# Holding the matmul engine's instructions of a hybrid decoder layer to the order of the source

## The chip, the cores and the metric

One core of a Trainium2 chip runs the whole kernel. The metric is the device time of one execution in microseconds (us). The engines are called as the profile calls them: PE (matrix products; PEld is its weight load), DVE (vector), ACT (scalar), POOL (GpSimd) and SP, which here only issues DMA transfers. Each engine works through its own list of instructions in the order of that list, and waits by semaphores for others.

## The reference

One decoder layer, 1024 positions, width 1024, all in float32:

```
h    = rmsnorm(x)
proj = h @ w_in              # q, k, v of 8 forgetting heads, 8 forget logits,
                             # q, k, v of 8 stick-breaking heads
o_fox = softmax(q.k/8 + F[t] - F[s], s <= t) @ v,  F = cumsum(log sigmoid(forget logit + bias))
o_sb  = A @ v,  A[t,s] = sigmoid(z[t,s]) * prod_{s<j<t}(1 - sigmoid(z[t,j])),  z = q.k/8, s < t
x = x + concat(rmsnorm(o_fox), rmsnorm(o_sb)) @ w_out
u = causal_dwconv3(rmsnorm(x) @ w_up);  gate, val = split(u)
x = x + (silu(gate) * val) @ w_down
return rmsnorm(x)
```

## The kernel before, in words

Every float32 product is made of three matmuls on a high and a low part of each operand (`mm3`, lines 158 to 161). The high part is a rounded copy (mostly by ACT), the low part the difference (by DVE or POOL), so a product's three matmuls need work of two other engines first.

**Attention.** The 16 heads come two by two. For a block of 128 queries `score` (line 449) makes the products of q and k, in tiles `s` of up to 512 columns (lines 466 and 467; line 470 adds the causal mask on the diagonal). The pool of `s` has three buffers. For a forgetting head DVE reads the tile at line 475, adding the row `fbt` (the cumulated forget gate, fetched from DRAM at line 444), ACT takes the exponential, DVE the reciprocal of the sum (line 488) and POOL scales the weights `w` (line 489). For a stick-breaking head ACT makes two sigmoids (lines 480 and 481), DVE a running product (line 493) and POOL the weights (line 494). `trans` (line 497) turns 128x128 pieces of `w` on PE (line 505) into `tp`; ACT copies the high part (line 513, `ph` or `pth`) and DVE makes the low one (line 514, `pl` or `ptl`). `pv` (line 517) multiplies by v: pairs of matmuls, high (line 525) and low (line 526).

**What sets the order.** `attention_stream` (line 566) yields these pieces with a cost each; a second stream, `fill_stream` (line 661), yields the projections of later heads (`qk_unit`, whose products are lines 159 to 161 on `pj`, and `v_quarter`, lines 277 to 279), the forget gate and its scan (`forget_scan`, line 319, with eight small transposes at line 326, whose result goes to DRAM and comes back as `fbt`), and at the end `open_out` (line 620) and the forgetting heads' part of the out-projection (`fox_out`, line 639, products of `ogh` and `ogl` with the weights). The loop at lines 692 to 701 emits them interleaved: before an attention piece, so much of the fill as LEAD + RATE x (cost so far) allows. `open_out` spreads the group norm (`group_spread`, line 601) and loads the attention outputs of the forgetting heads (`load_og`, line 607: ACT line 616, DVE line 617).

Emission is not yet the order in which an engine works. A scheduler of the framework orders the instructions of each engine afterwards, by its own estimate of when each is ready; only engines named in `manual_schedule` (line 72) keep the order of emission. Before, that is SP alone.

**After attention.** The rest of the out-projection and the second norm follow (`norm_cols`, line 744: sums of squares by matmuls of one column, line 748; `norm_rows`, line 754: `spread`, line 182, turns the reciprocal roots `rr` of line 175 into a row on PE at line 184, and ACT copies it to `rbc`). `first` and `second` (lines 829 and 834) make two products of the up-projection early for its first three blocks, emitted as first(0), `norm_cols`, `norm_rows`, first(1), first(2), second(0) to second(2). The up- and down-projection then take, block by block, seven products of sums of quarter matrices in place of eight (`product`, line 817; the loop at line 1059; the names in PORD), whose operands are made by DVE, POOL and ACT (`produce`, line 891, with the low part at line 906) a few products ahead. The final norm in three column parts is woven into the last products by `events` (line 1194).

Of the kernel before, what the change touches and what calls it, by code (L numbers as in the profile page):

```python
# [68 lines left out]
def layer(ctx, tc, xT, wqk, wv0, wv, wout, wup, wdn, cols, fbias, yT):  # L69
    nc = tc.nc  # L70
    act = nc.scalar.activation
    ctx.enter_context(tc.manual_schedule(engines={mybir.EngineType.SP}))

    const = ctx.enter_context(tc.tile_pool(name="const", bufs=1))
    dram = ctx.enter_context(tc.tile_pool(name="dram", bufs=1, space=DRAM))
# [1219 lines left out]
```

## Time and profile before

| | us |
|---|---|
| median of 3 runs | 1442.43 (1439.91 to 1442.75) |
| the profiled execution, its own time | 1441.58 |
| its span in the profile | 1439.6 |
| PE busy | 1317.6 (92%) |
| DVE busy | 1116.7 (78%) |
| POOL busy | 859.4 (60%) |
| ACT busy | 620.8 (43%) |

The span begins with the first instruction that the profile shows; the execution's own time is 2.0 us longer. Times in the rows below count from the span's start. The stretches of the kernel: the first norm and the first projections to about 81 us, attention to about 645, the rest of the out-projection and the second norm to about 740, the up-projection to about 1200, the down-projection and last norm to the end. The granted clock is the share of TensorE's full rate: 1.00 is 2.4 GHz and 0.50 is 1.2 GHz.

### The profile page before, as it was taken

What the parts mean: (1) busy time and instruction counts of PE and PEld (TensorE: products, weight loads), DVE (VectorE), ACT (ScalarE), POOL (GpSimd) and SP (SyncE); (2) the same over time, 40 slices, a digit from 0 to 9 for tenths busy, and PEclk for the clock granted to TensorE, in tenths of its full rate; (3) what the DMA queues carried; (4) which work ended last, traced back from release to release, by engine and by line L of the source; (5) the groups of instructions that cost most, each with busy time, mean ns of one, the idle gap of its engine ahead of it and who ended that gap; (6) DMA issues with size and microseconds to landing.
All of it is one profiled execution on the core that took longest, in us unless ns stands there. A gap on an engine that the chain in (4) does not pass through costs nothing.

```text
span 1439.6 us, 19147 instructions
## 1 busy us (share of the span) xinstructions
PE 1317.6 (92%) x6640; PEld 1075.9 (75%) x6640; DVE 1116.7 (78%) x1588; ACT 620.8 (43%) x1128; POOL 859.4 (60%) x730
## 2 busy tenths in 40 slices
PE   7899999999898887889778899999999998999995
PEld 5878878877787765777556688888888865878785
DVE  6246555655676677786899999998888889899987
ACT  5134434444454554353443434443443354344334
POOL 7344454543747573455667788878878763454423
PEclk9999999999999999999889999999999998999997
DMA  5556555545444454547311233333322355554313
GB/s 179 183 161 187 152 154 163 147 147 135 149 121 124 119 159 143 179 147 270 125 44 59 84 106 110 110 110 110 110 97 95 96 176 204 180 171 132 126 36 117
DMA packets 97232, 194.89 MB, mean 135 GB/s; under 512 B 8680, under 2 KB 35688, under 8 KB 97136
## 3 DMA queue, kind: packets, MB, share of 16 engines
q1 hardware_dynamic: 96272, 193.04, 42.6%
q8 instruction: 52, 0.85, 0.3%
q10 hardware_dynamic: 864, 0.64, 0.1%
q14 instruction: 44, 0.36, 0.1%
HBM read 132.79 MB, written 60.85 MB: 135 GB/s over the span
## 4 chain that ended last, share of the span: by engine, by line
PE 50%; DMA 18%; DVE 16%; POOL 7%; issue 6%; SPq 2%; ACT 2%; DVEq 0%; POOLq 0%; ACTq 0%
PE u L161 8%; PE u L160 8%; PE u L159 8%; PE pj L159 5%; PE pj L161 5%; PE pj L160 5%; DMA q<-qkd 4%; DVE fbt L493 3%; DMA vd<-vs 3%; DMA wraw<-in_wqk_dram 2%; DMA wraw<-in_wv_dram 2%; PE tp L505 2%; DMA fbt<-nfd 2%; PE o L526 2%; PE o L525 1%
## 5 line engine op out<-in xcount | busy, mean ns | idle before, releaser
L143 POOL TENSOR_TENSOR wl<-wraw,wh 128x256 fp32r<-128x256 f32 (+2 forms) x134 | 125.3, 952 | 26.9 <-ACT wh L140 21.3
L494 POOL TENSOR_TENSOR w<-w,fbt 128x128 f32<-128x128 f32 (+3 forms) x64 | 90.1, 1417 | 84.4 <-DVE fbt L493 59.9
L904 ACT CAST wh<-s 128x512 fp32r<-128x512 f32 (+1 forms) x136 | 79.8, 591 | 125.7 <-POOL s L879 71.0
L493 DVE TENSOR_TENSOR_SCAN fbt<-fbt 128x128 f32<-128x128 f32 (+3 forms) x64 | 103.5, 1624 | 25.9 <-ACT fbt L480 22.0
L142 POOL TENSOR_SCALAR wh<-wraw 128x256 fp32r<-128x256 f32 (+1 forms) x112 | 55.3, 509 | 108.8 <-DMA wraw<-in_wqk_dram 60.7
L878 POOL TENSOR_TENSOR s<-wraw 128x512 f32<-128x512 f32 (+1 forms) x34 | 55.8, 1641 | 96.0 <-DVE wl L906 53.5
L505 PE MATMUL tp<-ident,w 128*128 128x128 f32 x576 | 94.0, 281 | 19.5 <-DVE pl L514 9.5
L159 PE MATMUL pj<-xh,wh 128*128 128x512 f32 x224 | 103.1, 460 | 5.1 <-DVE yf L293 5.1
L906 POOL TENSOR_TENSOR wl<-wraw,wh 128x512 fp32r<-128x512 f32 x60 | 102.9, 1722 | 0.6 <-ACT wh L904 0.6
L505 PEld LDWEIGHTS tp<-ident,w 128*128 128x128 f32 x576 | 70.7, 144 | 39.1 <-DVE pl L514 12.6
L906 POOL TENSOR_TENSOR wl<-s,wh 128x512 fp32r<-128x512 f32 x48 | 88.5, 1845 | 13.8 <-ACT wh L904 13.4
L514 DVE TENSOR_TENSOR pl<-tp,ph 128x512 fp32r<-128x512 f32 x96 | 64.9, 685 | 40.9 <-ACT ph L513 40.5
L161 PE MATMUL pj<-xh,wl 128*128 128x512 f32 x224 | 91.9, 410 | 0.0
L160 PE MATMUL pj<-xl,wh 128*128 128x512 f32 x224 | 91.3, 407 | 0.0
L485 ACT ACTIVATE w<-w,m 128x128 f32<-128x128 f32 (+3 forms) x64 | 49.7, 776 | 91.1 <-DVE m L475 86.0
L1003 DVE SCALAR_TENSOR_TENSOR tg<-ua,col,tg 128x1023 f32<-128x1023 f32 (+1 forms) x44 | 88.1, 2002 | 0.0
L480 ACT ACTIVATE fbt<-s 128x512 f32<-128x512 f32 (+2 forms) x96 | 47.8, 498 | 83.8 <-PE s L470 39.2
L489 POOL TENSOR_SCALAR w<-w,l 128x128 f32<-128x128 f32 (+3 forms) x64 | 47.6, 748 | 59.9 <-DVE l L488 32.7
L904 ACT CAST wh<-wraw 128x512 fp32r<-128x512 f32 (+1 forms) x96 | 55.1, 589 | 63.1 <-DMA wraw<-in_wdn_dram 25.0
L1003 DVE SCALAR_TENSOR_TENSOR tv<-ub,col,tv 128x1023 f32<-128x1023 f32 (+1 forms) x44 | 76.0, 1727 | 5.7 <-ACT tv L1001 5.6
L513 ACT CAST ph<-tp 128x512 fp32r<-128x512 f32 x96 | 55.7, 590 | 53.1 <-PE o L525 33.4
L885 POOL TENSOR_TENSOR s<-wraw 128x512 f32<-128x512 f32 (+1 forms) x34 | 56.4, 1658 | 35.7 <-DVE wl L906 33.4
(409 smaller groups left out, 4569.4 us busy)
## 6 DMA issues: line engine op xcount, KB each, us to landing
wraw<-in_wup_dram SPq DMA_DIRECT2D x47, 512.0 KB, 3.6
qkd<-hl SPq DMA_DIRECT2D x32, 512.0 KB, 2.9
td<-tg SPq DMA_DIRECT2D x44, 256.0 KB, 2.3
vd<-vs SPq DMA_DIRECT2D x32, 256.0 KB, 4.5
q<-qkd SPq DMA_DIRECT2D x16, 512.0 KB
kh<-qkd SPq DMA_DIRECT2D x32, 256.0 KB, 16.6
kl<-qkd SPq DMA_DIRECT2D x32, 256.0 KB, 17.4
vt<-vd SPq DMA_DIRECT2D x16, 512.0 KB, 17.9
```

Of the source, the lines that this page charges most:

```text
L143: nc.gpsimd.tensor_tensor(self.lo[:, sl], self.raw[:, sl], f32(self.hi[:, sl]), ALU.subtract)
L159: nc.tensor.matmul(ps, ah, bh, start=start, stop=False)
L160: nc.tensor.matmul(ps, ah, bl, start=False, stop=False)
L161: nc.tensor.matmul(ps, al, bh, start=False, stop=stop)
L493: nc.vector.tensor_tensor_scan(qt[:, rev], qt[:, rev], qt[:, rev], 1.0, ALU.mult, ALU.bypass)
L494: nc.gpsimd.tensor_tensor(w[:, :n], w[:, :n], qt[:, T - n + 1:T + 1], ALU.mult)
L505: nc.tensor.transpose(tp[:, a * 256 + b * P:a * 256 + (b + 1) * P], ws[2 * g + b][:, kb * P:(kb + 1) * P], ident)
L514: nc.vector.tensor_tensor(pl[:, z:], tp[:, z:], f32(ph[:, z:]), ALU.subtract)
L885: nc.gpsimd.tensor_tensor(d["s3"], g[:, :w], v[:, :w], ALU.subtract)
L904: nc.scalar.copy(h[:, o:o + w], src)
L906: eng.tensor_tensor(l[:, o:o + w], src, f32(h[:, o:o + w]), ALU.subtract)
L1003: nc.vector.scalar_tensor_tensor(t[:, s:], us[:, :T - s], col[:, cw + tap:cw + tap + 1], t[:, s:], op0=ALU.mult, op1=ALU.add)
```

## The change

PE is added to the engines whose instructions keep the order in which the source emits them. No instruction is added or removed; SP's list is the same; the lists of DVE, ACT and POOL, which the scheduler still orders, shift at many places.

```diff
-    ctx.enter_context(tc.manual_schedule(engines={mybir.EngineType.SP}))
+    ctx.enter_context(tc.manual_schedule(engines={mybir.EngineType.SP, mybir.EngineType.PE}))
```

The first place is on PE at the start of attention, where the value projection (lines 277 to 279) begins; `s` are score tiles and `tp` the turned weights. Before:

```order
L467 MATMUL s<-kl,q 128x384
L470 LDWEIGHTS identb
L470 MATMUL s<-mask_f,identb 128x128
L159 MATMUL pj<-xh_239,wh 128x512
L160 MATMUL pj<-xl_247,wh 128x512
L161 MATMUL pj<-xh_239,wl 128x512
L277 MATMUL pj<-wh,xh_232 128x256
L278 MATMUL pj<-wl,xh_232 128x256
L279 MATMUL pj<-wh,xl_240 128x256
```

And in the changed kernel:

```order
L467 MATMUL s<-kl,q 128x384
L470 LDWEIGHTS identb
L470 MATMUL s<-mask_f,identb 128x128
L466 MATMUL s<-kh,q 128x512
L467 MATMUL s<-kl,q 128x512
L470 LDWEIGHTS identb
L470 MATMUL s<-mask_f,identb 128x128
L159 MATMUL pj<-xh_239,wh 128x512
L160 MATMUL pj<-xl_247,wh 128x512
L161 MATMUL pj<-xh_239,wl 128x512
L505 MATMUL tp<-ident,w 128x128 x3
L277 MATMUL pj<-wh,xh_232 128x256
```

The fourth score tile (512 columns wide) now follows the third one directly, and the first three transposes come ahead of the value projection; before, both came after 26 matmuls of it.

The second place is on PE a little later, and stands for 24 places like it in attention: four score matmuls between two of the pairs of lines 525 and 526.

```order
 L525 MATMUL o<-ph,vt 128x256
+L526 MATMUL o<-pl,vt 128x256
+L525 MATMUL o<-ph,vt 128x256
+L526 MATMUL o<-pl,vt 128x256
+L525 MATMUL o<-pth_576,vt 128x256
+L526 MATMUL o<-ptl_577,vt 128x256
+L525 MATMUL o<-pth_576,vt 128x256
+L526 MATMUL o<-ptl_577,vt 128x256
 L466 MATMUL s<-kh,q 128x384
 L467 MATMUL s<-kl,q 128x384
 L466 MATMUL s<-kh,q 128x256
 L467 MATMUL s<-kl,q 128x256
```

The four score matmuls stood right behind the first high product; now all eight matmuls of the pairs come ahead of them.

The third place is on PE in the second norm: `sq` are the squares whose sums go before, `b21h` an operand of the first up-projection products, `rr` the reciprocal roots.

```order
 L748 MATMUL u<-ones,sq 128x1
-L161 MATMUL pj<-b21h_7184,wl 128x512
-L159 MATMUL pj<-b21h_7186,wh 128x512
-L160 MATMUL pj<-b21l_7187,wh 128x512
-L161 MATMUL pj<-b21h_7186,wl 128x512
-L159 MATMUL pj<-b21h_7188,wh 128x512
-L160 MATMUL pj<-b21l_7189,wh 128x512
-L161 MATMUL pj<-b21h_7188,wl 128x512
 L184 MATMUL u<-ident,rr 128x128 x4
```

Seven matmuls (and two more between the sums, further up) no longer stand ahead of the spread of `rr`; they come behind the products `first(1)` and `first(2)`.

## Rows read from the trace of the kernel before

**Rows 1.** The page: span; busy time of the engines.
```profile
span 1439.6 us, 19147 instructions
PE 1317.6 (92%) x6640; PEld 1075.9 (75%) x6640; DVE 1116.7 (78%) x1588; ACT 620.8 (43%) x1128; POOL 859.4 (60%) x730
```

**Rows 2.** Stretches: length; busy PE, PEld, DVE, ACT, POOL; granted clock, DMA share, GB/s.
```profile
480.00:520.00 40.00, 37.40 (x199) 30.60 (x200) 26.20 (x34) 18.72 (x40) 30.52 (x30) 0.91 0.49 136
520.00:560.00 40.00, 27.27 (x162) 21.36 (x161) 33.74 (x37) 22.79 (x47) 17.87 (x12) 0.95 0.53 159
720.00:760.00 40.00, 29.85 (x100) 20.43 (x98) 36.74 (x41) 17.91 (x31) 28.41 (x13) 0.83 0.12 40
```

**Rows 3.** Waits of PE: line waiting, its releaser, total us, times, longest.
```profile
PE o L526 <- DVE pl L514: 11.5, 7, 3.2
PE s L466 <- DMA kh<-qkd: 7.1, 1, 7.1
```

**Rows 4.** Timeline of PE: start us, us, instruction, [idle before <-releaser].
```profile
73.02 0.77 PE L159 MATMUL pj<-xh,wh 128*128 128x512 f32 x1 [5.06 <-DVE yf L293]
...
93.30 0.33 PE L466 MATMUL s<-kh,q 128*128 128x384 f32 x1
...
94.47 0.27 PE L277 MATMUL pj<-wh,xh 128*128 128x256 f32 x1
...
97.41 0.28 PE L278 MATMUL pj<-wl,xh 128*128 128x256 f32 x1
98.68 0.51 PE L466 MATMUL s<-kh,q 128*128 128x512 f32 x1 [0.99 <-DVE m L475]
...
101.28 0.55 PE L505 MATMUL tp<-ident,w 128*128 128x128 f32 x3
```

**Rows 5.** Timelines of DVE and of POOL, 98 to 101 us.
```profile
98.32 0.29 DVE L475 CUSTOM_DVE_ANT_0 w<-s,fbt 128x128 f32<-128x128 f32 x1 [2.96 <-DMA fbt<-nfd]
...
100.75 1.04 POOL L489 TENSOR_SCALAR w<-w,l 128x256 f32<-128x256 f32 x2 [0.29 <-DVE l L488]
```

**Rows 6.** Stretches of PE alone: length, PE busy us, granted clock, DMA share, GB/s.
```profile
74.00:78.00 4.00, 4.00 (x11) 0.50 0.85 279
96.00:101.00 5.00, 4.01 (x27) 1.00 1.00 267
559.00:563.00 4.00, 4.00 (x19) 0.50 0.17 54
```

**Rows 7.** Timeline of PE around the first pairs of lines 525 and 526.
```profile
106.24 0.34 PE L466 MATMUL s<-kh,q 128*128 128x384 f32 x1
...
106.83 0.32 PE L526 MATMUL o<-pl,vt 128*128 128x256 f32 x1
```

**Rows 8.** Timeline of PE at the first scores of the new head.
```profile
558.31 1.08 PE L466 MATMUL s<-kh,q 128*128 128x256 f32 x3 [7.12 <-DMA kh<-qkd]
```

**Rows 9.** Chain that ended last: start us, us, what.
```profile
540.50 17.61 DMA kh<-qkd
```

**Rows 10.** Timelines of PE and of DVE at the second norm's spread.
```profile
721.63 1.05 PE L184 MATMUL u<-ident,rr 128*128 128x128 f32 x4
...
719.92 0.16 DVE L175 TENSOR_TENSOR rr<-rs_s,rs_t 128x4 f32<-128x4 f32 x1
723.34 3.59 DVE L765 SCALAR_TENSOR_TENSOR x<-x,col,rbc 128x512 f32<-128x512 f32 x2 [3.26 <-ACT rbc L757]
```

**Rows 11.** Timeline of PE at the start of the up-projection.
```profile
760.86 0.64 PE L161 MATMUL pj<-t4h,wl 128*128 128x512 f32 x1 [3.02 <-POOL wl L906]
```

**Rows 12.** Timelines of PE and DVE, down-projection and last norm.
```profile
1207.79 0.79 PE L160 MATMUL u<-b22l,wh 128*128 128x512 f32 x1 [1.08 <-POOL b22l L761]
...
1411.30 0.28 PE L161 MATMUL pj<-b21h,wl 128*128 128x256 f32 x1
...
1413.78 0.60 PE L184 MATMUL pj<-ident,rr 128*128 128x128 f32 x4
...
1413.48 0.15 DVE L175 TENSOR_TENSOR rr<-rs_s,rs_t 128x4 f32<-128x4 f32 x1
```

## Prediction

> **What bounds the kernel now.** I read the page first: of a span of 1439.6 us the matmul engine (PE) is busy 1317.6 [rows 1], so it idles 122 us, and nothing that only fills those waits better or worse can be worth more. I then cut the span into stretches of 40 us [rows 2]. In attention PE idles a little (2.6 us of 40 at 480); from 720 to 760 it is busy 29.85 and VectorE (DVE) 36.74, so there DVE is the bound. The list of what PE waited for [rows 3] says that the large sums belong to attention: the low halves of the weights that line 514 makes on DVE (11.5 us), and one wait of 7.1 us for a key transfer. PE starts its matmuls one after the other, so a waiting one holds all that stand behind it. A change of PE's order alone can therefore act in two ways only: it moves work out of a wait, or into one.
>
> The order of instructions says where PE's order differs: six pieces at the start of attention (A), 24 small swaps through attention (B), ten pieces around the opening of the out-projection (C), and then one spot each in the second norm (D), the start of the up-projection (E), the first block of the down-projection (F) and the end (G). No instruction is added or dropped, and SP's order is the same; DVE, ScalarE and POOL are still ordered by the framework and shift somewhat in response.
>
> **A, the first scores.** A score tile has three buffers. Before, the third score starts at 93.30, and then 26 matmuls of the value projection run from 94.47 to 97.53, one every 0.118 us; only after a wait of 0.99 us comes score four, at 98.68 [rows 4], because DVE begins on the first score at 98.32, held by the transfer of the forget row [rows 5]. Now score four stands directly behind score three, ahead of three projection matmuls of line 159 to 161, and the first three transposes stand ahead of the 26. So PE stops at about 93.7 and goes on at 98.68: 5.0 us. Score four and the three matmuls take about 1.3 us, to 100.0. The transposes cannot start sooner than at 101.28, as before, since POOL's weights for them come from 100.75 on [rows 5]: another 1.3 us. Together 6.3 us of waiting in place of 0.99, so **+5.3 us**; the 3 us of value projection are still owed afterwards. Two early scores no longer stand between the transposes of the forget scan (line 326), so the forget row may set out up to 0.6 us sooner (two scores of two steps of 0.118 each, and their masks), which makes it **+4.7**. Then the clock: after the 5.06 us wait that ends at 73.02 [rows 4], PE's granted clock from 74 to 78 was 0.50, that is 1.2 GHz, over 4.00 us of work [rows 6], half of which, 2.0, is loss. The 0.99 us wait lies in a stretch with a granted clock of 1.00. The bounds are +3 (the lower value with later waits taking some back) and +7.3 (5.3 + 2.0). I take **+5**, nearer the wait that is counted than the clock that may or may not fall. The Trainium skill (TensorE: Matmul & The Clock Gate, section HAM oscillation) says that a wait between bursts sets the array back to half rate, so that the next burst starts cold. By that rule alone A would be near +7 and the forecast 2 us later; the traced 5.06 us wait agrees with it, the 0.99 us wait shows no such loss.
>
> **B, the 24 swaps.** Before, scores of the next group were pulled in among the pairs of lines 525 and 526: at 106.24 four of them, until 106.83, stand between a high product and its low one [rows 7], 0.59 us of work beside DVE's making of the low half. Now the pairs come first and the scores behind, so what was hidden is waited for: at most 24 x 0.6 = 14.4 us, at least 0 where the low half was there already. The 11.5 us for line 514 [rows 3] say that even with this cover the low half is often late, which speaks for the upper end. Against it stands that PE has 2.6 us in 40 of further waits [rows 2], about 28 us over the 440 us of attention ahead of C, of which those on transfers and other engines shrink when PE comes later. I take four tenths, **+6**, with 0 and +14.4 kept for the range. The Trainium skill (Perfetto Trace Analysis, section Optimization Strategy) says that interleaving regimes with different limits can improve performance. Taken at its word, every swap that takes scores out from among the pairs loses its cover, and B would be +14.4; that the waits of line 514 exist in spite of the cover agrees, and no row shows that all of it is lost.
>
> **C, the opening of the out-projection.** Before, 24 products (24 x 0.235 = 5.6 us, twice the step of 0.118, being twice as wide) were spread through the last group of the old head, and then three scores of the new head waited 7.12 us for their keys [rows 8], with 16 pair matmuls and 11 transposes of the old head queued behind them. The transfer took 17.61 us on the chain [rows 9]; its start depends on SP, not on PE. Now the old head comes first, then the 24 products with the old head's rest, then the new scores. What moves in front of the wait is the 16 + 11, about 27 x 0.118 = 3.2 us with a transpose taken like a matmul of 256 columns, and the clock behind the wait (0.50 over 4.00 us [rows 6]) could give 2 more: **-5.2** at best. At worst the 24 products no longer cover the old head's waits on DVE, whose scans and low halves hold it at 33.74 of 40 there [rows 2]: **+5.6**. These two are the same size and I have no row that parts them: **0**.
>
> **D, the second norm.** Before, nine matmuls of the product second(0) were pulled ahead; seven of them stand between the sums and the spread of the reciprocal roots, which starts at 721.63 although DVE has it at 720.08 [rows 10]. DVE waits 3.26 us for what follows, until 723.34, and is the bound there. In the source's order the spread comes first, about 1.4 us sooner: **-1.4**. The nine, 9 x 0.235 = 2.1 us, come later, in a stretch in which PE idles 10 us of 40 [rows 2]; without that cover D would be +0.7.
>
> **E, the up-projection's start.** Before, PE took up the next block's third operand and waited 3.02 us for POOL's weights [rows 11]. Now the remaining products of the first block come first; their low halves come from DVE, which is the bound there [rows 2]. Between -3.0 (the wait gone) and +2.8 (twelve matmuls later, uncovered): **0**.
>
> **F and G.** In F, two matmuls of the next product, pulled ahead, covered part of a wait that still lasted 1.08 us until 1207.79 [rows 12]; uncovered they cost 0.9, and with the later ones up to 2. I take **+1**. In G the last norm's spread stands earlier, directly behind the matmul that starts at 1411.30; DVE has its operand at 1413.63, and it ran at 1413.78 [rows 12]. PE would stand for up to 2.1 us; but the tail waits for DVE as well: **+1**, between 0 and 2.1.
>
> **The sum.** 5 + 6 + 0 - 1.4 + 0 + 1 + 1 = +11.6 us. Against the profiled execution's own 1441.58 us this gives 1453.2; the median of the runs, 1442.43, lies 0.85 above it, less than this sum can resolve. I predict **1453**. A difference of 0.2%, 2.9 us, is about what a measurement of this kernel can tell from none.
>
> **The rivals.** *Faster:* the wait for the keys at 551 to 558 is the single place that decides. If the 24 products and the 3.2 us of the old head fill it rather than leave holes before it, C gives -5.2; with E's 3.0 gone, D's 1.4, B at 0, A at its lower bound of 3, and F and G at +1 together, the sum is 3 - 5.2 - 3 - 1.4 + 1 = -5.6, so 1436. For it: a wait of 7.12 us with work stuck behind is the sort of thing that the source's order avoids. Against it: the products had been covering DVE's waits. It decides from the point where the holes ahead of the keys are under 3 us. Chance 0.24. *No difference:* B is taken back by later waits, C gives 2 to 3, A costs its lower bound: 3 - 2.5 - 1.4 + 2 = +1, about 1443. Chance 0.16. *Much slower:* B whole, A 7.3, C +5.6: 14.4 + 7.3 + 5.6 - 1.4 + 2 = +27.9, about 1470; it wants all covers lost together, 0.08, and is part of the slower side. That the change does nothing is excluded: PE's order differs in 1053 lines.
>
> **How the numbers follow.** Forecast (slower by 3 to 22 us) 0.52, much slower 0.08, no difference 0.16, faster 0.24. So faster 0.24, within 0.2% 0.16, slower 0.60. The range runs from 1437, which leaves about 0.1 of the fast side out, to 1465, just past A and B at their upper bounds with C at 0 (7.3 + 14.4 + 0.6 = 22.3, or 1464); the forecast's own range is 1445 to 1464.
>
> **What would show it.** A: two waits on PE between 93 and 102 of about 5 and 1 us, on line 475's buffer and line 489's weights, perhaps with a clock at 0.50 behind them. B: the sum of PE's waits at line 526 for line 514 above 11.5 + several us, and the stretches from 120 to 520 each 0.5 us longer. C: the 7.1 us wait for keys smaller, and new waits at line 505 or 526 around 535 to 550. D: DVE's wait before the second norm's product 1.4 us shorter. E: the 3.02 us wait gone. The forecast is wrong if PE's waits for line 514 do not grow, or if the stretch from 520 to 640 gets shorter by more than 4 us.

## The result, and the profile after

The changed kernel takes **1462.11 us** (median of 4 runs, 1459.64 to 1465.86) against 1442.59 us for the kernel before beside it (1439.91 to 1444.29): a ratio of **1.0129**, 95% interval 1.0098 to 1.016. That is 14 to 23 us slower; forecast were 1453 us and a range of 1437 to 1465.

The page of the changed kernel, span and busy times:

```profile
span 1459.7 us, 19133 instructions
PE 1319.1 (90%) x6640; PEld 1076.9 (74%) x6640; DVE 1119.1 (77%) x1588; ACT 620.6 (43%) x1128; POOL 855.4 (59%) x730
```

Against [rows 1] the span grew by 20.1 us and PE's busy time by 1.5. So PE does the same work for practically the same time, and 18.6 us are idle time that was not there before. The list of what PE waited for, first of the changed kernel and then of the one before (line and what it waited for, total us, times, longest), says on whom:

```profile
PE tp L505 <- DVE pl L514: 14.7, 10, 3.8
PE o L526 <- DVE ptl L514: 12.4, 15, 2.5
PE o L526 <- DVE pl L514: 10.3, 10, 2.9
PE o L525 <- ACT pth L513: 6.9, 7, 2.4
PE s L466 <- DVE m L475: 4.7, 1, 4.7
```

```profile
PE tp L505 <- DVE pl L514: 9.5, 9, 2.0
PE o L526 <- DVE ptl L514: 3.9, 6, 1.9
```

With the row for `pl` at line 526 [rows 3] the waits for line 514 were 24.9 us before and are 37.4 now; those for line 513's `pth` at line 525 are new, and one wait at a score is 4.7 us where it was 1.0. The 7.1 us for the keys [rows 3] are gone. The stretches that answer to [rows 2] (PE, PEld, DVE, ACT, POOL, granted clock, DMA share, GB/s):

```profile
480.00:520.00 40.00, 36.07 (x189) 28.98 (x189) 26.54 (x32) 19.05 (x42) 27.36 (x28) 0.91 0.56 150
520.00:560.00 40.00, 28.29 (x154) 21.50 (x152) 31.71 (x34) 23.81 (x48) 20.08 (x14) 0.87 0.55 153
720.00:760.00 40.00, 26.10 (x98) 19.73 (x98) 33.72 (x34) 16.97 (x32) 26.36 (x17) 0.80 0.25 80
```

A stretch of the clock no longer holds the same work, so these say little beyond the granted clock, which fell in the last two. To find where the time went I compared the same matmul in both traces: at places where both lists have done the same work so far, the n-th matmul of PE is the same one, and its start after less its start before is the delay so far. At the head of A it is 1.0 us (a matmul of line 159 at 92.59 before and 93.59 after), behind A 7.3 (the matmul of line 277 at 103.94 in the trace of before):

```profile
103.94 0.36 PE L277 MATMUL pj<-wh,xh 128*128 128x256 f32 x1
```

```profile
111.20 0.28 PE L277 MATMUL pj<-wh,xh 128*128 128x256 f32 x1
```

The growth of this delay from place to place, for the changed kernel and for all further kernels below, each against the trace of before (us; places by the times of before; bold where PE was held there):

| kernel | A 93-104 | B 104-526 | C 526-645 | D 705-745 | E 745-860 | F 1200-1214 | G 1411-1427 |
|---|---|---|---|---|---|---|---|
| the changed kernel | **6.3** | **1.7** | **8.9** | **-1.4** | **-0.6** | **4.9** | **3.4** |
| e1_attention | **4.2** | **3.8** | **6.1** | 0.0 | 0.0 | 0.6 | 0.6 |
| e2_rest | 0.0 | 3.1 | 3.3 | **-1.4** | **-0.5** | **5.7** | **1.9** |
| e3_start_free | 0.7 | **6.0** | **5.5** | **-1.4** | **-0.7** | **5.7** | **1.8** |
| e4_open_free | **6.6** | **4.5** | -1.0 | **-1.5** | **-0.6** | **4.2** | **3.3** |
| k0_again (before itself) | 0.0 | 0.9 | 2.7 | 0.0 | -0.1 | 1.5 | 0.6 |
| e5_up_only | 0.0 | 0.9 | -0.2 | **-1.4** | **-0.6** | 1.0 | 0.8 |
| e6_row_early | **0.1** | **4.6** | **8.9** | **-2.1** | **-0.7** | **5.0** | **1.8** |
| e7_products_early | **4.7** | **6.5** | **10.9** | **-1.4** | **-0.5** | **5.1** | **1.8** |
| e8_low_first | **6.6** | **4.9** | **1.4** | **-1.4** | **-0.7** | **5.3** | **1.8** |
| e9_best | 1.7 | 0.1 | -0.7 | **-1.5** | **-0.4** | 1.4 | 0.0 |
| e10_swaps | 1.6 | **3.5** | -1.3 | 0.0 | -0.1 | 2.0 | 0.0 |
| e11_best_low_first | -0.7 | -1.3 | -0.2 | **-1.4** | **-0.5** | 0.9 | 0.7 |

The rows where PE was free show how far one and the same order drifts between executions and chips: under 0.2 us in D and E, up to 2 in F and up to 3.3 in B and C; in A e9_best and e11_best_low_first, whose lists are the same on every engine until 556 us, stand 2.4 us apart. A row does not add up to the whole: from 860 to 1200 every kernel, k0_again too, is 1.4 to 3.2 us faster than the first trace of before, and the other stretches left out differ by -1.7 to 3.2. In the experiments the kernel before ran between 1440.5 and 1453.9 us, so each of them is compared with it by the ratio alone. Ratios are given as recorded and are not the quotients of the medians beside them: four executions of 2521 to 4410 us (two of the kernel before, one each of e3_start_free and e9_best) are left out of the ratios and of that range, not of the medians; without its own e3_start_free's median is 1456.22.

### The profile page after: what moved, and what is told of

The parts are those of the page before. It is cut to its first block, busy times and chain, and to the rows that moved or that the text cites. A ratio compares the mean times of both kernels' runs of the same rounds, so it can differ in the third digit from the quotient of the medians.

```text
span 1459.7 us, 19133 instructions
## 1 busy us (share of the span) xinstructions
PE 1319.1 (90%) x6640; PEld 1076.9 (74%) x6640; DVE 1119.1 (77%) x1588; ACT 620.6 (43%) x1128; POOL 855.4 (59%) x730
## 4 chain that ended last, share of the span: by engine, by line
PE 49%; DVE 19%; DMA 15%; issue 6%; POOL 6%; ACT 3%; SPq 1%; DVEq 0%; POOLq 0%; ACTq 0%
PE u L160 8%; PE u L161 8%; PE u L159 7%; PE pj L159 5%; PE pj L160 4%; PE pj L161 4%; DVE fbt L493 3%; DMA wraw<-in_wqk_dram 3%; DMA q<-qkd 2%; PE tp L505 2%; POOL wl L143 2%; DMA wraw<-in_wv_dram 2%; PE o L526 2%; DMA fbt<-nfd 2%; DVE tg L1003 2%
## 5 line engine op out<-in xcount | busy, mean ns | idle before, releaser
L878 POOL TENSOR_TENSOR s<-wraw 128x512 f32<-128x512 f32 (+1 forms) x34 | 57.7, 1698 | 101.8 <-DVE wl L906 75.8
L505 PEld LDWEIGHTS tp<-ident,w 128*128 128x128 f32 x576 | 70.2, 144 | 40.8 <-DVE pl L514 20.1
L906 POOL TENSOR_TENSOR wl<-s,wh 128x512 fp32r<-128x512 f32 x48 | 80.6, 1680 | 16.1 <-ACT wh L904 10.0
L277 PE MATMUL pj<-wh,xh 128*128 128x256 f32 (+1 forms) x256 | 78.7, 308 | 0.7 <-DVE yf L293 0.7
```

The costliest lines, as they stand in the source:

```text
L277: nc.tensor.matmul(ps[:, :n], xh[k][:, sl], h, start=(k == 0), stop=False)
L505: nc.tensor.transpose(tp[:, a * 256 + b * P:a * 256 + (b + 1) * P], ws[2 * g + b][:, kb * P:(kb + 1) * P], ident)
L906: eng.tensor_tensor(l[:, o:o + w], src, f32(h[:, o:o + w]), ALU.subtract)
```

## The experiments

A region can hold PE to the source's order for a part of the program: `hold_pe()` opens one, `held.close()` ends it. Where PE is not held, its list is that of before, except where another edit moves it (the start of e9 and e11, C in e11).

**e1_attention, e2_rest: which half?**

```diff
-    fill_to(10.0)
+    hold_pe(); fill_to(10.0)
...
-    box = {}
+    held.close(); box = {}
```

> PE is held to the source's order from the first head to the end of attention only; behind it the order of before. By the traces the same matmuls run 1.0 us later than before at the head of A, 7.3 at its end, 9.0 at the head of C and 17.9 at the end of attention. Theory (each place adds its own delay to a matmul engine that is never ahead): +17 us, 1459 to 1461. Rival (what attention loses is given back where the vector engine is the bound, 720 to 835 us): under +12, 1454 or less.

Measured: 1457.93 us against 1446.03, ratio 1.0084 (1.0062 to 1.0106), about 12 us. In the second kernel the region opens where this one closes and lasts to the end:

```diff
-    box = {}
+    hold_pe(); box = {}
```

> PE is held from the end of attention on only. Theory (adds up): the rest of the 20 us, +2 to +4, out of about -3 through the up-projection, +5 at the start of the down-projection and +2 to +4 at the end; 1444 to 1447. Rival (attention's loss was partly given back, so the rest costs more by itself): +6 or more, 1449 or above.

Measured: 1449.69 against 1446.03, ratio 1.0022 (1.0003 to 1.004), about 3 us. The halves make 15 us, near the lower end of the whole (14 to 23). That attention is the larger part is shown. The first kernel's time lies at the edge of what the rival expected, and the theory's 17 us lie outside its interval (9 to 15); its trace, 15.7 us late at the last matmul, sides with the delays adding up: it gets nothing back between 705 and 860 (0.0 in D and in E).

**e3_start_free, e4_open_free: A and C taken out.** The region opens at the thirteenth piece of the attention stream; in the other kernel it is closed at `open_out` and opened again behind attention.

```diff
-    for cost, f in attention_stream():
-        fill_to(LEAD + RATE * ta)
+    for n_, (cost, f) in enumerate(attention_stream()):
+        fill_to(LEAD + RATE * ta); n_ == 12 and hold_pe()
```

> Held everywhere but in A, the first scores. Theory (A is a loss of 6.3 us that nothing takes back): 6 us under the changed kernel, 1455 to 1457. Rival (later waits on other engines had shrunk because A made PE late, and grow again without it): less than 3 us under it, 1459 to 1462.

Measured: 1457.75 against 1446.03, ratio 1.0065 (1.0044 to 1.0086).

```diff
-        yield 0, open_out
+        yield 0, lambda: (held.close(), open_out())
...
-    box = {}
+    hold_pe(); box = {}
```

> Held everywhere but from the opening of the out-projection to the end of attention (C and the four swaps behind it). Theory (the loss of 8.9 us from 526 to 646 us is made there): 8 to 10 us under the changed kernel, 1452 to 1455. Rival (it is the late arrival of PE from A and B that costs there, by transfers and the vector engine's scans falling otherwise): less than 4 us under it, 1458 or more.

Measured: 1461.18 against 1446.03, ratio 1.0102 (1.0068 to 1.0135). With the whole at 1.0129, freeing A is worth 0.64% (9 us), beyond the intervals, and freeing C 0.27% (4 us), within them. By the time alone e4's rival did no worse than its theory of 8 to 10 us. The table is sharper, though each trace is one execution, and e4's the fastest of its four: A grows by 0.7 in place of 6.3, C by -1.0 in place of 8.9. By it the rival of e4, that C costs because PE comes late, falls: there PE comes 13.4 us late to C and loses nothing.

**k0_again: the kernel before as a control.**

> The kernel before, unchanged, as a control on the chip that runs the next three: its trace says how far the same order of work drifts between executions. Any theory: the same as before within 5 us, and by place (start of attention, 104 to 526, 526 to 645, the rest) within 3 us of the first trace of before.

Measured: 1448.05 us, once; by place within 2.7 us of the first trace. The list of every engine is word for word that of before, so this is drift alone, and the yardstick for the table.

**e5_up_only: the gains alone.** PE held from the end of attention to the end of the up-projection.

```diff
-    box = {}
+    hold_pe(); box = {}
...
-    up.close()
+    up.close(); held.close()
```

> PE is held only from the end of attention to the end of the up-projection (D and E); free before and behind. The traces with D and E held give -1.4 between 705 and 745 us and -0.6 between 745 and 860, whatever stands ahead. Theory (D's earlier spread is a gain that lasts): 2 to 4 us under the kernel before on the same chip, ratio 0.997 to 0.9985. Rival (the 3.7 us that E loses at 774 are given back only by what stands behind it in the fully held kernels): within 1 us of before, or above.

Measured: 1444.39 against 1445.49, ratio 0.9986 (0.9968 to 1.0003): not told apart from no change by the time; the trace repeats D and E to 0.1 us.

**e6_row_early: what A waits for.** The loads of v and of the forget row for the first head are emitted four units of fill earlier, ahead of a store (line 238) that waits on SP. PE's list is word for word that of the changed kernel.

```diff
-    load_head(0, 0)
+    load_head(0, 0); fill_to(LEAD - 4.0); load_v(0, 0)
...
-        yield 0, partial(load_v, 0, 0)
```

> PE held everywhere; the loads of the first head's v and forget row are emitted 4 units of fill earlier, which puts them ahead of one store (line 238) on SP that waits until 91.7 us; PE's order is that of the changed kernel word for word. Theory (A is the arrival of the forget row, exposed by the score that now stands in front): the row lands 3 to 4 us sooner, the wait of 4.70 us at the fourth score falls to about 1.5, the clock does not fall, and the time is 4 to 6 us under the changed kernel, 1456 to 1458. Rival (POOL's and ACT's chain behind the scores sets the start of the transposes): the wait moves to line 505 and less than 2 us are won.

Measured: 1460.38 against 1445.49, ratio 1.0092 (1.0059 to 1.0125); 0.37% under the whole, with intervals that overlap. PE's timeline decides, of the changed kernel and then of this one:

```profile
94.38 0.33 PE L466 MATMUL s<-kh,q 128*128 128x384 f32 x1
...
99.66 0.79 PE L466 MATMUL s<-kh,q 128*128 128x512 f32 x1 [4.70 <-DVE m L475]
...
102.46 0.90 PE L505 MATMUL tp<-ident,w 128*128 128x128 f32 x3
```

```profile
94.59 0.49 PE L466 MATMUL s<-kh,q 128*128 128x512 f32 x1 [0.56 <-DVE m L475]
96.44 0.55 PE L505 MATMUL tp<-ident,w 128*128 128x128 f32 x3 [0.29 <-POOL w L489]
```

SP issues the forget row at 88.27 in place of 92.66 (its timeline, changed kernel first):

```profile
92.66 1.06 SPq L444 DMA_DIRECT2D fbt<-nfd  x1
```

```profile
88.27 0.33 SPq L444 DMA_DIRECT2D fbt<-nfd  x1
```

The wait shrinks from 4.70 to 0.56 us, PE's granted clock is 1.00 from 96 to 105 us, and A costs 0.1 in place of 6.3 with the same list on PE. So A is the row's arrival, no longer covered by 26 matmuls; the rival's wait at line 505 is 0.29.

**e7_products_early: are C the holes that the products had filled?**

```diff
-LAG, LEAD, RATE, PAUSE, TRC = 3, 40.0, 1.327, 12.0, 0.67
+LAG, LEAD, RATE, PAUSE, TRC = 3, 40.0, 1.327, 4.0, 0.67
```

> PE held everywhere; PAUSE is 4 in place of 12, so that the forgetting heads' out-projection products are emitted earlier, among the old head's last groups, nearer to where the scheduler had put them (the first at 3078 of PE's list, 3141 in the changed kernel). Theory (C is the old head's holes that the products had covered): the stretch from 526 to 645 us of before's time loses 4 to 5 us less, 1457 to 1459. Rival (the products then wait for their operands and hold PE; C lies in the swaps of the last heads, behind the products): no gain, 1460 to 1466.

Measured: 1469.03 against 1445.49, ratio 1.0151 (1.0118 to 1.0185), C 10.9. Products emitted this early do not help PE over C. The placement overshoots: the first of them is matmul 2987 of PE's list (matmuls alone counted), against 3010 before and 3045 in the changed kernel, so it does not exclude that products at their old places would help. The ratio, 1464 us beside the first median of before, is what the rival forecast.

**e8_low_first: DVE's list.** The traces show a wait of 3.84 us in C where PE's list is the same before and after. PE's timeline of before, then of the changed kernel:

```profile
594.35 0.60 PE L505 MATMUL tp<-ident,w 128*128 128x128 f32 x4
597.49 0.79 PE L159 MATMUL pj<-ogh,wh 128*128 128x512 f32 x1 [2.54 <-DVE t L652]
...
598.93 1.06 PE L505 MATMUL tp<-ident,w 128*128 128x128 f32 x4
```

```profile
605.01 0.60 PE L505 MATMUL tp<-ident,w 128*128 128x128 f32 x4
607.10 0.50 PE L159 MATMUL pj<-ogh,wh 128*128 128x512 f32 x1 [1.49 <-DVE t L652]
...
611.90 1.11 PE L505 MATMUL tp<-ident,w 128*128 128x128 f32 x4 [3.84 <-DVE pl L514]
```

And DVE's timeline of before, then of the changed kernel:

```profile
596.74 0.69 DVE L652 TENSOR_TENSOR t<-pj,rbc 128x512 f32<-128x512 f32 x1 [1.03 <-DMA x2d<-t]
597.35 0.68 DVE L514 TENSOR_TENSOR pl<-tp,ph 128x512 fp32r<-128x512 f32 x1
597.99 1.30 DVE L653 TENSOR_TENSOR t<-xin,t 128x512 f32<-128x512 f32 x2
```

```profile
606.35 0.69 DVE L652 TENSOR_TENSOR t<-pj,rbc 128x512 f32<-128x512 f32 x1 [2.75 <-DMA x2d<-t]
606.96 1.75 DVE L493 TENSOR_TENSOR_SCAN fbt<-fbt 128x768 f32<-128x768 f32 x1
608.63 2.61 DVE L653 TENSOR_TENSOR t<-xin,t 128x512 f32<-128x512 f32 x2
611.16 1.27 DVE L514 TENSOR_TENSOR pl<-tp,ph 128x512 fp32r<-128x512 f32 x2
```

Before, the low half (line 514), which frees the buffer of the turned weights, came right behind line 652. The scheduler, planning around the held PE, put a running product and two additions ahead of it. The experiment raises the priority of line 514 from `open_out` on; PE's list stays word for word that of the changed kernel.

```diff
-        nc.vector.tensor_tensor(pl[:, z:], tp[:, z:], f32(ph[:, z:]), ALU.subtract)
+        with (tc.high_priority(offset=200) if "og" in fill else ExitStack()): nc.vector.tensor_tensor(pl[:, z:], tp[:, z:], f32(ph[:, z:]), ALU.subtract)
```

> PE held everywhere, its list word for word that of the changed kernel; the scheduler is told to prefer the low halves of line 514 from the opening of the out-projection on, which puts DVE's list back near that of before at a few spots (the low half ahead of the two additions of line 653). Theory (a good part of C is not PE's order at all but DVE's list, which the scheduler planned anew: the wait of 3.84 us at line 505 stands where PE's list is the same in both kernels): that wait falls under 2.5 us and the stretch from 600 to 620 us of before's time loses 1 us in place of 3.3; 2 to 3 us under the changed kernel in all. Rival (PE arrives there later and meets DVE's transfers at another time): the wait stays above 3.

Measured: 1458.4 against 1447.67, ratio 1.0068 (1.0054 to 1.0081), below the whole's interval. The wait in PE's timeline of this kernel:

```profile
609.85 0.66 PE L505 MATMUL tp<-ident,w 128*128 128x128 f32 x4 [1.28 <-DVE pl L514]
```

It is 1.28 in place of 3.84 us, since on DVE the low half now comes ahead of the two additions (DVE's timeline of this kernel):

```profile
607.46 1.75 DVE L493 TENSOR_TENSOR_SCAN fbt<-fbt 128x768 f32<-128x768 f32 x1
609.12 0.67 DVE L514 TENSOR_TENSOR pl<-tp,ph 128x512 fp32r<-128x512 f32 x1
```

C costs 1.4 in place of 8.9, but not all of that is the edit's. The lists of all engines are those of the changed kernel until 608 us, and by then, at the matmul that starts at 597.49 before and 607.10 in the changed kernel, C had grown by -2.5 here and 0.6 there: 3.1 us of drift (e1_attention, with the same lists, had -1.8). Behind that matmul C grows by 6.9 to 8.3 in the four kernels that hold it with the changed kernel's list (it, e1, e3, e6), by 3.9 here, and by -0.1 to 2.8 where PE is free with the list of before. So the edit takes about 4 of some 7 us, though from 600 to 620 the delay grew by about 2.5, not by the 1 that I expected. PE from that matmul to the end of C, before, in the changed kernel and here (length, busy, granted clock, DMA share, GB/s):

```profile
597.50:644.90 47.40, 43.75 (x247) 0.97 0.46 152
607.10:662.80 55.70, 46.75 (x247) 0.91 0.41 134
607.60:658.90 51.30, 43.18 (x247) 1.00 0.45 144
```

The same 247 matmuls take 3.6 us less here than in the changed kernel, at the higher clock; the rest is fewer waits. In k0_again the clock of this stretch was 0.91 too, so its share cannot be put down to the edit alone. That DVE's list makes the wait is shown, from one run with one edit: it is 3.84 us in e1 and e3 too and 3.45 in e6, and 1.28 here. What makes the rest of C is not.

**e9_best, e10_swaps, e11_best_low_first.** The ninth joins e5 and e6:

> The gains alone: PE held from the end of attention to the end of the up-projection, as in the run before, and the loads of the first head's forget row ahead of the store on SP. Theory: D and E give -2 and the earlier row the 1 us that PE waits at the fourth score before; 3 us under the kernel before, ratio 0.997 to 0.9985. Rival (a row that comes earlier only lets PE run into the next wait, on POOL's weights): no more than the 0.9986 of the run with D and E alone.

Measured: 1444.35 against 1447.67, ratio 0.9981 (0.9966 to 0.9996). Where PE is free the earlier row did not show: A grew by 1.7 us and the delay was back to 1.6 at 150. Inconclusive for the row, faster in all, with an interval that ends at 0.9996. The tenth holds PE only in B (opened as in e3, closed at `open_out`):

> PE is held only from behind A to the opening of the out-projection: the swaps B alone. By the traces that held them they cost 1.7 to 6.5 us there, by those that did not, 0 to 3. Theory (covers lost, half of them taken back): +2 to +5 over the kernel before. My forecast of +6 would put it at +6 or more; the rival that later waits take everything back, within 1.

Measured: 1453.14 against 1447.67, ratio 1.0037 (1.0018 to 1.0057), some 5 us (2.6 to 8.2): the rival, within 1, falls, and the forecast of 6 or more is not parted from the theory's 2 to 5. In its trace B grows by 3.5 us, and A by 1.6, where its lists are those of before: drift. The eleventh adds e8's edit to e9:

> As the run with the gains alone, and the low halves of line 514 are preferred from the opening of the out-projection on. Theory (DVE's list matters there with PE free too): 1 to 2 us under that run. Rival (the scheduler's own list was already good where PE is free to fill): the same within 1 us or slower.

Measured: **1441.31 us against 1447.67, ratio 0.9954** (0.9941 to 0.9966). This version beats both kernels, by 5 to 9 us the one before. The source's order is kept only where it wins (D and E), and DVE's list is told what PE waits for. That this preference is what wins here is not shown: against e9_best its trace gains 2.4 us in A and 1.4 in B, where the lists of the two are the same, and loses 0.5 in C, where they differ.

## Why the prediction was right, step by step

The sign, the range and the main reasoning held: PE idles more, PE's busy time is the same, and the changed order moves more waits into the open than it closes. In size I was short, 11.6 of 19.5 us, and the sum hides two terms that failed. That the time still lies inside the range is partly luck: its upper end allowed for A and B at their worst, and what came was more from C and F than either was given.

- **A: forecast 5 (3 to 7.3), measured 4.2 to 6.6 where held.** Right in the main step: stop at the fourth score forecast 93.7 to 98.68, traced 94.96 to 99.66, and e6 shows the cause. Two sub-steps were off, and their errors nearly cancel. The second wait of 1.3 us at line 505 did not come, because score four and the three matmuls ran at the lower clock and took 2.8 us; and the row, issued at 92.66, is 0.6 us sooner against a PE that is 1.0 us late, as forecast, but took 6.51 us on the chain and let DVE begin at 99.31, which against that same 1.0 is no sooner than 98.32 [rows 5]. The clock did fall. A stretch of PE in the changed kernel (length, busy, granted clock, DMA share, GB/s):

```profile
100.00:105.00 5.00, 4.94 (x18) 0.50 0.93 199
```

4.94 us at a granted 0.50 (1.2 GHz) are 2.5 lost, about the 2.0 that I kept for the upper bound. The Trainium skill (TensorE: Matmul & The Clock Gate, section HAM oscillation) says that behind a wait for a transfer the next burst starts cold. The trace agrees, with a granted 0.50 behind the 4.70 us wait, which the row's transfer caused.

- **B: forecast 6 (0 to 14.4).** Kernels that held PE there grew by 1.7 to 6.5, mean 4.4, those that did not by -1.3 to 3.1, mean 0.6 with the trace of before as zero: about 3.8. The mechanism is only in part the forecast one. From A to C PE's waits at line 526 for the low half are 11.8 to 14.4 us in the kernels that held B and 11.1 to 12.6 in the others. New is a wait at line 525 for the high half that ACT copies (line 513), which I had not named: 3.2 us in each of the eight that held B and none in the other six. Before, scores had stood ahead of the high product as well, behind the transposes, and covered that copy. From e10_swaps (106.8 to 532.3):

```profile
PE o L525 <- ACT pth L513: 3.2, 4, 2.0
```

One swap of the forecast kind, which lies in C, before and after:

```profile
577.00 0.38 PE L525 MATMUL o<-pth,vt 128*128 128x256 f32 x1
...
578.17 0.39 PE L526 MATMUL o<-ptl,vt 128*128 128x256 f32 x1 [0.24 <-DVE ptl L514]
...
587.26 0.58 PE L526 MATMUL o<-pl,vt 128*128 128x256 f32 x1 [2.58 <-DVE pl L514]
```

```profile
587.26 0.28 PE L525 MATMUL o<-pth,vt 128*128 128x256 f32 x1
589.82 0.39 PE L526 MATMUL o<-ptl,vt 128*128 128x256 f32 x1 [2.28 <-DVE ptl L514]
...
599.32 0.39 PE L526 MATMUL o<-pl,vt 128*128 128x256 f32 x1 [0.24 <-DVE pl L514]
```

Before, a score's rest and a product run between the first two; now PE stands 2.28 us. Ten microseconds later the wait of 2.58 us for the next low half is down to 0.24, so this swap is wholly taken back: between 575 and 590 the delay grows by 3.3 us and shrinks by 3.6. In all the waits at line 526 rose from 15.4 to 22.7 us, as the forecast asked, most of it in C; what share the 24 swaps get back was not measured.

- **C: forecast 0 (-5.2 to +5.6), measured about 7: this step failed.** Without e7 and e8, kernels that held PE there grew by 5.5 to 8.9, mean 7.4; those that did not, with the trace of before as zero, by 0.3 in the mean. The opening itself came out near the forecast 0: the 7.1 us wait for keys went, as I said it could, and the holes of the old head came, 10.4 us of waits between 535 and 563 where there had been 3.6 beside the keys. Of these, in the changed kernel (535 to 563):

```profile
PE o L525 <- ACT pth L513: 3.3, 2, 2.4
PE o L526 <- DVE pl L514: 3.3, 2, 2.9
```

Up to the matmul at 597.49 C had grown by -1.8 to 0.8 in the four that held it (changed kernel, e1, e3, e6). The loss, 6.9 to 8.3 us, lies behind it, and there I had priced nothing beyond the swaps of B. I priced only PE's list; I had written that DVE's list shifts in response and gave it no cost. By e8 it makes the wait of 3.84 us, and with the clock that goes along about 4 of the 7; the other 3 stay open, and are little more than the drift that free kernels show there.

- **D: forecast -1.4, measured -1.4 or -1.5 in nine of the ten kernels that held it, -2.1 in one, 0.0 in the three that did not.** PE waits for the roots at the spread, and DVE for what follows 1.83 us where it was 3.26 [rows 10]:

```profile
737.10 1.12 PE L184 MATMUL u<-ident,rr 128*128 128x128 f32 x4 [1.50 <-DVE rr L175]
736.88 0.16 DVE L175 TENSOR_TENSOR rr<-rs_s,rs_t 128x4 f32<-128x4 f32 x1
738.87 3.57 DVE L765 SCALAR_TENSOR_TENSOR x<-x,col,rbc 128x512 f32<-128x512 f32 x2 [1.83 <-ACT rbc L757]
```

- **E: forecast 0 (-3.0 to +2.8), measured -0.6.** The 3.02 us wait [rows 11] is replaced by a larger one, and later ones shrink. By 774 the delay had grown from 15.5 to 19.2 us, by 835 it was 14.0. Between the two PE's waits fell from 4.3 to 1.2 us, and the same 233 matmuls took 54.38 us in place of 56.48, at a granted clock of 1.00 in place of 0.97. The larger wait:

```profile
780.29 0.79 PE L161 MATMUL u<-t3h,wl 128*128 128x512 f32 x1 [5.12 <-DVE wl L906]
```

- **F: forecast 1 (to 2), measured about 4 (4.2 to 5.7 where held, 0.6 to 2.0 elsewhere): mis-sized.** I priced the two matmuls ahead of the first low half. The seven behind it had covered the second low half as well, which stands bare now. PE's timeline of before at that second low half, then that of the changed kernel at both:

```profile
1211.95 0.40 PE L160 MATMUL u<-b22l,wh 128*128 128x512 f32 x1
```

```profile
1221.04 0.79 PE L160 MATMUL u<-b22l,wh 128*128 128x512 f32 x1 [2.21 <-POOL b22l L761]
...
1225.01 0.80 PE L160 MATMUL u<-b22l,wh 128*128 128x512 f32 x1 [2.32 <-DVE b22l L761]
```

Against 1.08 at the first [rows 12] and no wait at the second, that is 3.5 us more of waits.

- **G: forecast 1 (0 to 2.1), measured 1.8 to 3.4 where held, 0 to 0.8 elsewhere.** The spread waits 1.94 us:

```profile
1432.08 0.65 PE L184 MATMUL pj<-ident,rr 128*128 128x128 f32 x4 [1.94 <-DVE rr L175]
```

Of the rivals, the faster one asked for fewer than 3 us of holes ahead of the keys and for B near 0; both failed. The one of no difference wanted B taken back, 2.5 us from C and A at its lower bound; none of the three came. The much slower one had C's upper end about right, and B far too high.

## What to carry to other kernels

Ask of each reordered stretch what the moved instructions had covered, down to the second and third wait behind them, and compare the delay of the same instruction along both traces; a total tells little where gains and losses lie side by side. Trust a place only as far as kernels with the same lists agree there. Holding one engine makes the scheduler plan the others anew: read their lists too, at the places where the held engine waits for them. Here the order fixed by hand paid where PE was not the bound and a short chain was (D), and cost in most other places, so fix it place by place and not throughout.

## What was not expected

- The same list on PE with a preference for line 514's low halves, which changes DVE's list in 23 places, ACT's in 10 and POOL's in 4, moved the time by 0.6% (1.0129 to 1.0068), as much as the whole start of attention. Its trace places about half of that.
- A loss of 3.7 us by 774 (E) was given back with interest 60 us later, three fifths by shorter waits and the rest by the clock.
- The order of before, where it was kept, differed from its first trace by up to 3.3 us in C and 3.1 in B, though PE was busy 1317.6 and 1316.9 us in the two traces of that kernel; effects of that size cannot be read from one trace there. In the last part of C the difference is the clock: k0_again's stretch there has 46.68 us of PE at a granted 0.91, against 43.75 at 0.97 in the first trace.
